# Rotary latent queries of two head groups from one product of 512 columns instead of two products of 256

## The chip, the cores and the metric

The kernel runs on one core of a Trainium2 chip, as one launch. The metric is the device time of that launch in microseconds (us); lower is better. The engines are named as in the profile: PE does matmuls (PEld is its loading of the stationary operand), DVE is the vector engine, ACT the activation engine, POOL and SP issue transfers here and do little else. Each engine works through its own queue in order, and semaphores order the queues among each other.

## The reference

A decoder trunk of four layers over 256 tokens of width 2048, in float32. Layers 0 and 3 use multi-head latent attention, layer 1 a sparse attention with an indexer, layer 2 a windowed attention with sinks. Every layer has one input projection, four memory cross-attention heads of width 256, a SiLU gate over the whole branch of 3072 columns, and one output projection that is added to the residual. What matters here is the query side of the latent layers:

```python
c_q, c_kv, k_rope, mq, gate = _split(h @ w_in, [A_Q_LORA, A_KV_LORA, A_ROPE, MEM_WIDTH, BRANCH_WIDTH])
q = (_rmsnorm(c_q, q_norm) @ w_uq).reshape(B, S, A_HEADS, A_NOPE + A_ROPE)      # 16 heads of 128 + 64
kv = (_rmsnorm(c_kv, kv_norm) @ w_ukv).reshape(B, S, A_HEADS, A_NOPE + A_V)     # 16 heads of 128 + 128
q_nope, q_rope = q[..., :A_NOPE], _rope(q[..., A_NOPE:])
s = (einsum('bqhd,bkhd->bhqk', qn, k_nope) + einsum('bqhd,bkd->bhqk', qr, k_rope)) * scale
```

`A_Q_LORA` is 1536, so the query projection runs over 12 feature tiles of 128. Of the 192 columns of `w_uq` of each head the first 128 are plain, the last 64 are rotated by position (`_rope`).

## The kernel before

Float32 products are made of three products in PE's faster 32-bit format (`float32r`): every operand is split into a high part and the remainder, and high by high, high by low and low by high are summed in PSUM. Weights are loaded by SP in `stage` (one of five buffers `wr`), then split in `parts_of`: ACT copies the high part `wh` (line 60), DVE subtracts for the low part `wl` (line 64), three buffers each. Two functions make the products:

- `rows_by` (lines 234 to 236): the activations are stationary, the weights move; the result has tokens on the partitions and up to 512 columns. Six matmuls per feature tile: two row tiles of 128 tokens by three products.
- `columns_by` (lines 253 and 257): the weights are stationary, the activations move.

A latent layer first builds the compressed queries and keys (`first`: acc_kva, acc_kvb, acc_cq; the result is `cT`). Then it goes through six parts in the order 4, 0, 1, 2, 3, 5: parts 4 and 5 are memory heads (`memory_project`, `memory_attend`), parts 0 to 3 are groups of four latent heads. For a group g, `project(g)` makes in this order

1. the rotary queries acc_qr (`rows_by`, 12 feature tiles, 4 heads x 64 = 256 columns), which DVE rotates from PSUM (`rope`, lines 508 to 511, with the single buffer `rot`), ACT and DVE split into `qrs` (a single buffer), PE transposes (line 370, tile `tr`) and ACT copies to `qrT`,
2. the plain queries acc_qn (two halves by `columns_by`, evacuated by `head_parts`), 
3. the keys acc_kn (two halves), the values acc_va (`rows_by`, 512 columns),
4. the group's quarter of the gate, acc_g (two halves by `columns_by` over 16 feature tiles).

`attend` then makes for each of the four heads the scores (line 625, tile `sp`; the rotary part `sp<-kr,qrT` is among them), the softmax, its transposes (line 402, `ptp`) and the product with the values (lines 406 and 407, `o`). `w_out` of the part before follows (acc_wo, lines 234 to 236).

That is the program's order. The order on each engine's queue is set by a scheduler that runs at build time over a modelled timeline, and that moves pieces of one part among those of another: the softmax of one group lies among the first products of the next. Tiles come from pools with a tag and a number of buffers: accumulators `acc` (4, a product takes two), `aux` (3: `qrT`, the values `va`, the loaded memory values `mvr`, and others), `pq` (5), `wr` (5). POOL issues the loads `mvr` and `mkr` of stored memory values and keys. SP issues one transfer per feature tile for a column pattern with gaps, as for acc_qr (pieces of 64 floats, 256 B).

Of the kernel before, what the change touches and what calls it, by code (L numbers as in the profile page):

```python
# [8 lines left out]
F32 = mybir.dt.float32  # L9
F32R = mybir.dt.float32r  # L10
# [5 lines left out]
P = 128  # L16
S = 256
# [6 lines left out]
A_QL, A_KVL, A_ROPE, A_NOPE = 1536, 512, 64, 128  # L24
MEMW = 1024
ST = 2
N_TAB = 384
PQ, AUX, WR = 5, 3, 5


@with_exitstack
def kernel(ctx: ExitStack, tc: tile.TileContext, a: dict, out: bass.AP,
                             kinds=(0, 1, 2, 0)):
    nc = tc.nc
# [3 lines left out]
    act = ctx.enter_context(tc.tile_pool(name="act", bufs=1))  # L38
    wk = ctx.enter_context(tc.tile_pool(name="wk", bufs=1))
# [3 lines left out]
    def misc(name, dt=F32):  # L43
        return ps.tile([P, 512], dt, name=name, tag="mp", bufs=4)
# [8 lines left out]
    def f32(ap):  # L53
        return ap.bitcast(F32)
# [4 lines left out]
    def copy_act(o, i, scale=1.0):  # L59
        nc.scalar.activation(o, i, AF.Copy, scale=scale)  # L60

    def split(hi, lo, src):
        copy_act(hi, src)
        nc.vector.tensor_sub(lo, src, f32(hi))  # L64
# [135 lines left out]
    def stage(w, k0, m, cols):  # L200

        n = cols[1] if len(cols) == 2 else cols[1] * cols[4]
        wr = wp.tile([P, ST * 512], F32, name="wr", tag="wr", bufs=WR)
        src = w[k0 * P:(k0 + m) * P, :].rearrange("(k p) n -> p k n", p=P)
        dst = wr[:, :m * n].rearrange("p (k n) -> p k n", k=m)
        if len(cols) == 2:
            nc.sync.dma_start(dst, src[:, :, cols[0]:cols[0] + n])
        else:
            c0, r, step, off, width = cols
            for k in range(m):  # L210
                nc.sync.dma_start(dst[:, k, :].rearrange("p (r c) -> p r c", r=r),
                                  src[:, k, c0:c0 + r * step].rearrange("p (r c) -> p r c", r=r)
                                  [:, :, off:off + width])
        return wr, n

    def parts_of(wr, c0, n):
        wh = wp.tile([P, 512], F32R, name="wh", tag="wh", bufs=3)
        wl = wp.tile([P, 512], F32R, name="wl", tag="wl", bufs=3)
        split(wh[:, :n], wl[:, :n], wr[:, c0:c0 + n])
        return wh, wl  # L220

    def rows_by(xt, kts, w, k0, cols, name):

        acc = [ps.tile([P, 512], F32, name=f"acc_{name}{t}", tag="acc", bufs=4) for t in range(2)]
        for s in range(0, kts, ST):
            m = min(ST, kts - s)
            wr, n = stage(w, k0 + s, m, cols)
            for k in range(m):
                wh, wl = parts_of(wr, k * n, n)
                q = xt[(s + k) // 4]  # L230
                for t in range(2):
                    xh, xl = (q[:, v, (s + k) % 4, t * P:(t + 1) * P] for v in range(2))
                    first, last = s + k == 0, s + k == kts - 1
                    nc.tensor.matmul(acc[t][:, :n], xh, wh[:, :n], start=first, stop=False)  # L234
                    nc.tensor.matmul(acc[t][:, :n], xh, wl[:, :n], start=False, stop=False)  # L235
                    nc.tensor.matmul(acc[t][:, :n], xl, wh[:, :n], start=False, stop=last)  # L236
        return acc

    def columns_by(xt, kts, w, k0, cols, name):

        acc = [ps.tile([P, 2, S], F32, name=f"acc_{name}{j}", tag="acc", bufs=4) for j in range(2)]
        for s in range(0, kts, 2 * ST):
            m = min(2 * ST, kts - s)
            wr, n = stage(w, k0 + s, m, cols)
            for k2 in range(0, m, 2):
                wh, wl = parts_of(wr, k2 * S, 2 * S)
                for k in range(2):
                    kt = s + k2 + k
                    q = xt[kt // 4]

                    for j in range(2):
                        o = k * S + j * P
                        nc.tensor.matmul(acc[j], wh[:, o:o + P], q[:, :, kt % 4, :],  # L253
                                         start=kt == 0, stop=False)
                    for j in range(2):
                        o = k * S + j * P
                        nc.tensor.matmul(acc[j][:, 0, :], wl[:, o:o + P], q[:, 0, kt % 4, :],  # L257
                                         start=False, stop=kt == kts - 1)
        return acc

    def total(acc, name="z"):
        z = wk.tile([P, S], F32, name=name, tag="z", bufs=3)
        copy_act(z, acc[:, 1, :])
        nc.vector.tensor_add(z, z, acc[:, 0, :])  # L264
        return z
# [98 lines left out]
    def transposed(dst, srcs):  # L364

        for i0 in range(0, len(srcs), 4):
            i1 = min(len(srcs), i0 + 4)
            tp = misc("tr", F32R)
            for i in range(i0, i1):
                nc.tensor.transpose(tp[:, (i - i0) * P:(i - i0 + 1) * P], srcs[i], identr)  # L370
            copy_act(dst(i0, i1), f32(tp)[:, :(i1 - i0) * P].rearrange("p (j c) -> p j c", c=P))


    def gate(nm, w, c0):
        gT = act.tile([P, 4, S], F32, name="gT", tag="gT", bufs=2)
        for h in range(2):
            acc = columns_by(nm.at, 16, w, 0, (c0 + h * S, S), "g")
            for j in range(2):
                z = total(acc[j])
                hz = wk.tile([P, S], F32, name="hz", tag="z", bufs=3)  # L380
                nc.vector.tensor_mul(hz, z, nm.half)
                th = wk.tile([P, S], F32, name="th", tag="e", bufs=4)
                nc.scalar.activation(th, hz, AF.Tanh)
                nc.vector.scalar_tensor_tensor(gT[:, 2 * h + j, :], th, 1.0, hz, op0=OP.add, op1=OP.mult)
        return gT
# [117 lines left out]
    def rope(dst, src, t, n):  # L503

        cb = cos[:, t, None, :].to_broadcast([P, n, A_ROPE])
        q = A_ROPE // 2
        rot = wk.tile([P, 4, A_ROPE], F32, name="rot", tag="rot", bufs=1)[:, :n]
        nc.vector.tensor_mul(rot[:, :, :q], src[:, :, q:], sin[:, t, None, :q].to_broadcast([P, n, q]))
        nc.vector.tensor_mul(rot[:, :, q:], src[:, :, :q], sin[:, t, None, q:].to_broadcast([P, n, q]))
        nc.vector.tensor_mul(dst, src, cb)  # L510
        nc.vector.tensor_add(dst, dst, rot)


    class Latent:
# [6 lines left out]
        def first(self):  # L521
# [55 lines left out]
            for z, sg in zip(self.scale, (1.0, -1.0)):  # L577
                nc.vector.tensor_scalar(z, qr, sg * (A_NOPE + A_ROPE) ** -0.5, None, op0=OP.mult)

        def project(self, g):  # L580

            j = self.j
            wq, wkv = a["w_uq"][j], a["w_ukv"][j]
            qn, kn = [], []
            qr = act.tile([P, 4, S], F32R, name="qrT", tag="aux", bufs=AUX)
            v = act.tile([P, 2, 512], F32, name="va", tag="aux", bufs=AUX)
            acc = rows_by(self.cT[:3], 12, wq, 0, (g * 768, 4, 192, A_NOPE, A_ROPE), "qr")
            for t in range(2):
                rr = wk.tile([P, 4, A_ROPE], F32, name="qrr", tag="z", bufs=3)
                rope(rr, acc[t][:, :S].rearrange("p (h d) -> p h d", h=4), t, 4)  # L590
                rs = wk.tile([P, 4, 2, A_ROPE], F32R, name="qrs", tag="qrs", bufs=1)
                split(rs[:, :, 0, :], rs[:, :, 1, :], rr)
                transposed(lambda i0, i1: qr[:, i0:i1, t * P:(t + 1) * P],
                           [rs[:, h].rearrange("p a b -> p (a b)") for h in range(4)])
            for half in range(2):
                acc = columns_by(self.cT[:3], 12, wq, 0, (g * 768 + half * 384, 2, 192, 0, A_NOPE), "qn")
                q = act.tile([P, 2, 2, S], F32R, name="qn", tag="pq", bufs=PQ)
                head_parts(q, acc)
                qn.append(q)
            for half in range(2):  # L600
                acc = columns_by(self.cT[3:], 4, wkv, 0, (g * 1024 + half * 512, 2, 256, 0, A_NOPE), "kn")
                k = act.tile([P, 2, 2, S], F32R, name="kn", tag="pq", bufs=PQ)
                head_parts(k, acc)
                kn.append(k)
            acc = rows_by(self.cT[3:], 4, wkv, 0, (g * 1024, 4, 256, A_NOPE, A_NOPE), "va")
            for t in range(2):
                copy_act(v[:, t, :], acc[t])
            return qn, qr, kn, v, gate(self.nm, self.w, self.g0 + g * 512)

        def attend(self, qn, qr, kn, v, gT):  # L610
            y = act.tile([P, 2, 4, S], F32R, name="y", tag="y", bufs=2)
# [288 lines left out]
```

## Time and profile before

| what | us |
|---|---|
| median of 3 runs | 2638.45 (2636.72 to 2638.67) |
| the profiled execution's own time | 2637.23 |
| its span, from the first to the last instruction | 2635.0 |
| PE busy | 2605.1 |
| DVE busy | 1890.2 |
| ACT busy | 1625.5 |
| POOL busy | 57.8 |

The span is what the trace covers; the own time also holds what lies around it. Busy time of PE counts overlapping matmuls once. In the views, a row `L236 PE MATMUL acc_qr<-wh,cT` is line 236 of the kernel, the engine, the operation, and the tiles written and read; `x` stands ahead of a count, and in a view by order of time the first two numbers are the start and the duration in us. The product names of the text (acc_qr and so on) are those tiles.

### The profile page before, as it was taken

The numbers are of one execution on the slowest core, as the hardware profiler recorded it, in microseconds if no ns is written. First come the engines' busy times: TensorE is split into PE (matmuls) and PEld (weight loads), VectorE is DVE, ScalarE is ACT, GpSimd is POOL, SyncE is SP. The second block draws the span as 40 slices with busy tenths as digits, with TensorE's granted clock in tenths as the row PEclk, the third lists the DMA queues.
The fourth block names the chain that finished last, engine by engine and source line by source line (L and its number), as shares of the span: only waits on it lengthen the run. The fifth ranks groups of instructions, "written<-read, shape, count | busy, mean of one in ns | idle before, by whom it ended". The sixth has DMA issues, their size and how long they took to land.

```text
span 2635.0 us, 43048 instructions
## 1 busy us (share of the span) xinstructions
PE 2605.1 (99%) x14623; PEld 2260.1 (86%) x14623; DVE 1890.2 (72%) x4174; ACT 1625.5 (62%) x3460; POOL 57.8 (2%) x102
## 2 busy tenths in 40 slices
PE   8999999999999999999999999999999999999998
PEld 7888888888888889888888888888888888888886
DVE  7566656677767685877777776777778767776767
ACT  6455556556656566666666666676666655665655
POOL 1000000000000000000000000000000000000000
PEclk9999999999999999999999999999999999999999
DMA  7898886666557666565556665555555766665764
GB/s 268 272 290 275 273 265 199 165 187 168 169 160 224 192 189 171 167 183 170 175 164 190 188 191 176 173 172 177 191 168 162 206 163 188 165 171 156 226 183 135
DMA packets 454064, 507.50 MB, mean 193 GB/s; under 512 B 69300, under 2 KB 352180, under 8 KB 452692
## 3 DMA queue, kind: packets, MB, share of 16 engines
q1 hardware_dynamic: 439716, 446.42, 57.3%
q0 software_dynamic: 13120, 56.17, 6.7%
q8 instruction: 115, 1.88, 0.3%
q10 hardware_dynamic: 1008, 2.16, 0.2%
q14 instruction: 105, 0.86, 0.1%
HBM read 485.70 MB, written 31.56 MB: 196 GB/s over the span
## 4 chain that ended last, share of the span: by engine, by line
PE 97%; DMA 1%; DVE 1%; ACT 0%; issue 0%; ACTq 0%; POOLq 0%
PE acc_g L253 14%; PE acc_g L257 7%; PE acc_wo L234 7%; PE acc_wo L235 7%; PE acc_wo L236 7%; PE acc_mq L253 5%; PE acc_mk L253 5%; PE acc_qn L253 3%; PE acc_cq L253 3%; PE acc_mq L257 2%; PE acc_mk L257 2%; PE acc_q L234 2%; PE acc_q L235 2%; PE acc_q L236 2%; PE acc_mv L235 2%; PE acc_mv L236 2%
## 5 line engine op out<-in xcount | busy, mean ns | idle before, releaser
L64 DVE TENSOR_TENSOR wl<-wr,wh 128x512 fp32r<-128x512 f32 (+2 forms) x1776 | 1172.9, 663 | 642.9 <-ACT wh L60 612.7
L60 ACT ACTIVATE wh<-wr 128x512 fp32r<-128x512 f32 (+2 forms) x1776 | 1079.9, 609 | 846.1 <-PE acc_g L253 186.0
L253 PE MATMUL acc_g<-xT,wh 128*128 128x512 f32 x1536 | 488.9, 397 | 0.6 <-DVE z L264 0.6
L257 PEld LDWEIGHTS acc_g<-xT,wl 128*128 128x128 f32 x1536 | 285.2, 188 | 60.7
L257 PE MATMUL acc_g<-xT,wl 128*128 128x256 f32 x1536 | 311.0, 280 | 0.0
L235 PE MATMUL acc_wo<-wl,y 128*128 128x512 f32 x768 | 302.5, 394 | 0.6 <-DVE wl L64 0.5
L236 PE MATMUL acc_wo<-wh,y 128*128 128x512 f32 x768 | 299.1, 390 | 0.0
L253 PEld LDWEIGHTS acc_g<-xT,wh 128*128 128x128 f32 x1536 | 238.1, 189 | 4.7 <-issue 1.1
L234 PE MATMUL acc_wo<-wh,y 128*128 128x512 f32 x768 | 240.4, 393 | 0.7 <-ACT wh L60 0.6
L235 PEld LDWEIGHTS acc_wo<-wl,y 128*128 128x128 f32 x768 | 144.3, 188 | 30.0 <-DVE wl L64 1.4
L236 PEld LDWEIGHTS acc_wo<-wh,y 128*128 128x128 f32 x768 | 144.2, 188 | 28.4
L234 PEld LDWEIGHTS acc_wo<-wh,y 128*128 128x128 f32 x768 | 141.3, 188 | 27.8 <-ACT wh L60 1.0
L253 PE MATMUL acc_mk<-mT,wh 128*128 128x512 f32 x512 | 160.8, 396 | 1.4 <-ACT wh L60 1.4
L253 PE MATMUL acc_mq<-xT,wh 128*128 128x512 f32 x512 | 161.7, 397 | 0.0
L807 DVE TENSOR_TENSOR x<-x,acc_wo 128x512 f32<-128x512 f32 x192 | 125.5, 681 | 7.2 <-PE acc_wo L236 6.9
L253 PE MATMUL acc_qn<-cT,wh 128*128 128x512 f32 x384 | 123.2, 399 | 0.0
L253 PE MATMUL acc_cq<-xT,wh 128*128 128x512 f32 x384 | 120.8, 396 | 0.0
L257 PEld LDWEIGHTS acc_mk<-mT,wl 128*128 128x128 f32 x512 | 95.8, 188 | 22.7 <-DVE wl L64 0.4
L257 PEld LDWEIGHTS acc_mq<-xT,wl 128*128 128x128 f32 x512 | 93.7, 188 | 20.0
L257 PE MATMUL acc_mq<-xT,wl 128*128 128x256 f32 x512 | 102.5, 281 | 0.0
L235 PE MATMUL acc_q<-wl,xT 128*128 128x512 f32 x256 | 102.4, 400 | 0.0
L257 PE MATMUL acc_mk<-mT,wl 128*128 128x256 f32 x512 | 100.8, 278 | 0.0
(284 smaller groups left out, 4453.5 us busy)
## 6 DMA issues: line engine op xcount, KB each, us to landing
wr<-in_w_out_dram SPq DMA_DIRECT2D x192, 512.0 KB, 3.7
wr<-in_w_in_a_dram SPq DMA_DIRECT2D x176, 512.0 KB, 4.2
wr<-in_w_mem_kv_dram SPq DMA_DIRECT2D x128, 512.0 KB, 5.2
wr<-in_w_in_b_dram SPq DMA_DIRECT2D x112, 512.0 KB, 3.7
wr<-in_w_in_c_dram SPq DMA_DIRECT2D x104, 512.0 KB, 3.7
wr<-in_w_uq_dram SPq DMA_DIRECT2D x288, 128.0 KB, 2.8
tab<-flat POOLq DMA_DIRECT2D x8, 1536.0 KB, 10.9
wr<-in_w_in_a_dram SPq DMA_DIRECT2D x32, 288.0 KB, 3.0
```

The source lines that it names most:

```text
L60: nc.scalar.activation(o, i, AF.Copy, scale=scale)
L64: nc.vector.tensor_sub(lo, src, f32(hi))
L234: nc.tensor.matmul(acc[t][:, :n], xh, wh[:, :n], start=first, stop=False)
L235: nc.tensor.matmul(acc[t][:, :n], xh, wl[:, :n], start=False, stop=False)
L236: nc.tensor.matmul(acc[t][:, :n], xl, wh[:, :n], start=False, stop=last)
L253: nc.tensor.matmul(acc[j], wh[:, o:o + P], q[:, :, kt % 4, :], start=kt == 0, stop=False)
L257: nc.tensor.matmul(acc[j][:, 0, :], wl[:, o:o + P], q[:, 0, kt % 4, :], start=False, stop=kt == kts - 1)
L807: nc.vector.tensor_add(xs, xs, acc[t])
```

## The change

The rotary queries of two neighbouring groups (0 and 1, 2 and 3) are made by one call of `rows_by` with 8 heads x 64 = 512 columns per feature tile. It is a function of its own, `rotary`, which `project` calls for even groups, behind the plain queries, the keys and the values and ahead of the gate. Rotation, split, transposes and copies stay the same for each group and row tile. Two tiles `qrT` now live at once, and the pool `aux` has five buffers instead of three; a scratch for the descriptors of POOL's transfers is set to 8192 bytes.

```diff
-PQ, AUX, WR = 5, 3, 5
+PQ, AUX, WR = 5, 5, 5
...
+        def rotary(self, g):
+
+            self.qr = [act.tile([P, 4, S], F32R, name="qrT", tag="aux", bufs=AUX) for z in range(2)]
+            acc = rows_by(self.cT[:3], 12, a["w_uq"][self.j], 0, (g * 768, 8, 192, A_NOPE, A_ROPE), "qr")
+            for t in range(2):
+                for z in range(2):
+                    rr = wk.tile([P, 4, A_ROPE], F32, name="qrr", tag="z", bufs=3)
+                    rope(rr, acc[t][:, z * S:(z + 1) * S].rearrange("p (h d) -> p h d", h=4), t, 4)
+                    rs = wk.tile([P, 4, 2, A_ROPE], F32R, name="qrs", tag="qrs", bufs=1)
+                    split(rs[:, :, 0, :], rs[:, :, 1, :], rr)
+                    transposed(lambda i0, i1: self.qr[z][:, i0:i1, t * P:(t + 1) * P],
+                               [rs[:, h].rearrange("p a b -> p (a b)") for h in range(4)])
+
         def project(self, g):
...
-            qr = act.tile([P, 4, S], F32R, name="qrT", tag="aux", bufs=AUX)
             v = act.tile([P, 2, 512], F32, name="va", tag="aux", bufs=AUX)
-            acc = rows_by(self.cT[:3], 12, wq, 0, (g * 768, 4, 192, A_NOPE, A_ROPE), "qr")
-            for t in range(2):
-                rr = wk.tile([P, 4, A_ROPE], F32, name="qrr", tag="z", bufs=3)
-                rope(rr, acc[t][:, :S].rearrange("p (h d) -> p h d", h=4), t, 4)
-                rs = wk.tile([P, 4, 2, A_ROPE], F32R, name="qrs", tag="qrs", bufs=1)
-                split(rs[:, :, 0, :], rs[:, :, 1, :], rr)
-                transposed(lambda i0, i1: qr[:, i0:i1, t * P:(t + 1) * P],
-                           [rs[:, h].rearrange("p a b -> p (a b)") for h in range(4)])
...
             for t in range(2):
                 copy_act(v[:, t, :], acc[t])
-            return qn, qr, kn, v, gate(self.nm, self.w, self.g0 + g * 512)
+            if g % 2 == 0:
+                self.rotary(g)
+            return qn, self.qr[g % 2], kn, v, gate(self.nm, self.w, self.g0 + g * 512)
...
-    nc = _bacc.Bacc("TRN2", target_bir_lowering=False, num_devices=1)
+    nc = _bacc.Bacc("TRN2", target_bir_lowering=False, num_devices=1,
+                     dynamic_dma_scratch_size=8192)
```

## The prediction

> **What bounds the kernel now.** I read the page first, then the waits of PE, then the busy time of the two stretches in which the rotary queries lie (layers 0 and 3, the latent ones).
>
> ```profile
> span 2635.0 us, 43048 instructions
> PE 2605.1 (99%) x14623; PEld 2260.1 (86%) x14623; DVE 1890.2 (72%) x4174; ACT 1625.5 (62%) x3460; POOL 57.8 (2%) x102
> ...
> PE 97%; DMA 1%; DVE 1%; ACT 0%; issue 0%; ACTq 0%; POOLq 0%
> ```
>
> ```profile
> PE acc_kvb L234 <- ACT wh L60: 1.8, 1, 1.8
> PE o L786 <- ACT pT L60: 1.7, 3, 0.6
> ```
>
> ```profile
> core 0: us, PE busy (x) PEld busy (x) DVE busy (x) ACT busy (x) POOL busy (x), PEclk, DMA share, GB/s
> 395.00:940.00 545.00, 545.00 (x3176) 479.31 (x3176) 385.27 (x863) 331.77 (x698) 3.57 (x6) 1.00 0.64 183
> ```
>
> PE is busy 99% of the span, and 97% of the chain that ended last is PE. No single wait of PE after the first loads is longer than the 1.8 us on acc_kvb, early in layer 0, before any rotary query. In the 545 us from there to the end of layer 0 PE is busy in all 545.00, at a granted clock of 1.00. So in the stages that change there is no idle time to win, and whatever shortens PE's own list shortens the span one to one, as long as no other engine or transfer becomes late. Busy time counts overlapping matmuls as one, so the price of a matmul is read from start to start, in the order of time.
>
> **The products, which are the gain.** A latent layer has four head groups, two layers make eight. Before, each has 12 feature tiles x 2 row tiles x 3 products (high by high, high by low, low by high) of 256 columns:
>
> ```profile
> L234 PE MATMUL acc_qr<-wh,cT x192: 277/283/368, 519.9 to 2444.9; 128*128 128x256 f32 x192
> L235 PE MATMUL acc_qr<-wl,cT x192: 278/283/387, 520.1 to 2445.2; 128*128 128x256 f32 x192
> L236 PE MATMUL acc_qr<-wh,cT x192: 277/283/287, 520.2 to 2445.4; 128*128 128x256 f32 x192
> ```
>
> These are 576 matmuls. After, four calls of 72, which is 288 matmuls of 512 columns. The start-to-start time of the first kind is read where nothing else stands between; of the second kind acc_va is the nearest row: same function, same lines, same operand layout, 512 columns, weights in blocks from the same kind of load.
>
> ```profile
> 797.08 0.40 PE L234 MATMUL acc_qr<-wh,cT 128*128 128x256 f32 x2
> ...
> 799.96 0.63 PE L253 MATMUL acc_qn<-cT,wh 128*128 128x512 f32 x2
> ```
>
> ```profile
> 736.61 0.63 PE L234 MATMUL acc_va<-wh,cT 128*128 128x512 f32 x2
> ...
> 741.40 0.62 PE L253 MATMUL acc_g<-xT,wh 128*128 128x512 f32 x2
> ```
>
> From 797.08 to 799.96 stand 24 matmuls (four feature tiles of six): 2.88 / 24 = 0.120 us. From 736.61 to 741.40 stand 21: 4.79 / 21 = 0.228 us. So 576 x 0.120 = 69.1 us become 288 x 0.228 = 65.7 us: **-3.4 us**. Two halves cost 0.240 where one whole costs 0.228; one matmul of 256 saved is worth 12 ns. As the upper bound for 512 columns I take acc_g's pair among halves, 0.235 (0.47 us for two, from 760.20 on, below), which would leave -1.4 us; the other way, both intervals are read to 0.01 us over 20 and more matmuls, which is worth 0.3 us: -3.7 us.
>
> The second PE term is the stretch behind transposes and products in plain f32:
>
> ```profile
> 776.39 0.49 PE L402 MATMUL ptp<-ident,e 128*128 128x128 f32 x3
> 776.63 0.48 PE L235 MATMUL acc_wo<-wl,y 128*128 128x512 f32 x1
> 776.95 0.39 PE L236 MATMUL acc_wo<-wh,y 128*128 128x512 f32 x1
> ```
>
> The first matmul behind a group of ptp takes 0.32 to the next instead of 0.23. In the built order of the changed kernel the softmax of the group before is spread differently (its ptp, o and sp now fall among acc_qn and acc_kn), and there are 178 such places behind ptp for 180, equally many behind o (32) and behind transposes of rotary and other parts (78). 2 x 0.09: **-0.2 us**. PE's order outside the latent projections is the same instruction by instruction.
>
> Sum: **-3.6 us** on the profiled execution's 2637.23 us (2635.0 us span and 2.2 around it). That run lies 1.2 us under the median of the runs shown, 2638.45, to which the same difference applies: 2634.8 us, 0.14% less. A measurement of this kernel tells about 0.2%, 5.3 us, from no change.
>
> **What costs nothing, and what covers it.**
> - The splits of the weights: 96 pairs of 256 columns on ACT and DVE become 48 of 512, slightly less work on engines that are 62% and 72% busy; cover is PE.
> - The rotation. Still 16 calls, but four in a row instead of two, at the start of the gate, with single buffers `rot` and `qrs`. DVE shows how such a row runs in the kernel before:
>
> ```profile
> 800.22 0.28 DVE L508 TENSOR_TENSOR rot<-acc_qr,sin 128x128 f32<-128x128 f32 x1
> 800.42 0.28 DVE L509 TENSOR_TENSOR rot<-acc_qr,sin 128x128 f32<-128x128 f32 x1
> 800.62 0.41 DVE L510 TENSOR_TENSOR qrr<-acc_qr,cos 128x256 f32<-128x256 f32 x1
> 800.95 0.68 DVE L64 TENSOR_TENSOR wl<-wr,wh 128x512 fp32r<-128x512 f32 x1
> 801.55 0.42 DVE L511 TENSOR_TENSOR qrr<-qrr,rot 128x256 f32<-128x256 f32 x1
> ...
> 803.82 0.42 DVE L64 TENSOR_TENSOR qrs<-qrr,qrs 128x256 fp32r<-128x256 f32 x1
> 804.16 0.68 DVE L390 TENSOR_TENSOR yt<-o,gT 128x512 f32<-128x512 f32 x1
> ```
>
> ```profile
> 760.20 0.63 PE L253 MATMUL acc_g<-xT,wh 128*128 128x512 f32 x2
> 760.67 0.39 PE L257 MATMUL acc_g<-xT,wl 128*128 128x256 f32 x2
> 760.90 0.62 PE L253 MATMUL acc_g<-xT,wh 128*128 128x512 f32 x2
> ```
>
> From start to start a rotation and its split take 0.20 + 0.20 + 0.33 + 0.34 + 0.34 = 1.41 us of DVE, a split of weights 0.60. In the built order the first four transposes stand 34 gate matmuls behind the last rotary product, the next ones 22 to 24 apart; a gate matmul takes 0.70 / 4 = 0.175 us, so 5.9 us and then 3.9 to 4.2 us. DVE needs 4.0 us for the first (800.22 to 804.16, with four other pieces among them) and 1.41 + 3 x 0.60 = 3.2 us for each further one. It fits, with 0.7 us to spare at the tightest. In the kernel before, the first transposes also stand 34 matmuls behind, and PE does not wait there.
> - The accumulators: two pairs in all; the rotary pair is read until the fourth rotation (about 7.6 us of DVE), and the gate's second half, which takes that pair, comes 64 matmuls, 11 us, later.
> - SP's queue: the 96 issues of 128 KB become 48 of 256 KB, and stand behind those of kn and va instead of ahead of those of qn; bytes and pieces (256 B) stay the same.
> - POOL's queue: five `aux` buffers let the memory values `mvr` of some parts be issued earlier, by pairs; the smaller DMA scratch touches POOL's transfers alone, and POOL is busy for 57.8 us of the span. Loads that then collide with those of the weights have the five `wr` buffers as cover; without that the price is a wait like the 1.8 us on acc_kvb (below).
>
> **The rivals.**
>
> *The 256-byte pieces cannot keep pace* (slower). A feature tile now takes 6 x 0.228 = 1.37 us of PE for 256 KB, 192 GB/s, all in pieces of 256 B, for 12 tiles in a row.
>
> ```profile
> 776.00:778.00 2.00, 2.00 (x12) 1.65 (x11) 1.35 (x3) 1.28 (x3) 0.00 (x0) 1.00 0.57 128
> 778.00:780.00 2.00, 2.00 (x11) 1.66 (x10) 0.81 (x2) 1.11 (x2) 0.00 (x0) 1.00 0.58 131
> 510.00:511.00 1.00, 1.00 (x8) 0.91 (x7) 0.96 (x4) 0.90 (x3) 0.00 (x0) 1.00 1.00 227
> ```
>
> Over 2 us such pieces have gone at no more than 128 to 131 GB/s, but at a DMA share of 0.57 and 0.58, since the buffers asked for no more; in the one microsecond at a share of 1.00 it was 227. If 131 were the limit, 12 x 262 KB would take 24.0 us; the first load can be issued when the last one of qn is split, 11 us ahead of its use (kn and va), of which some 2 us go to splits that run ahead; the last of the six loads would land at about 2 + 24 = 26 us, and is wanted at 9.1 + 5 x 2.74 = 22.8 us: 3.2 us late, four times, 13 us, so 2634.8 + 13 = 2648 us. It decides below 3.15 MB / (22.8 - 2) = 151 GB/s. The 227 speaks against it. [...]
>
> *The chain of rotations ends late* (no gain). If ACT's half of the split or its copies come in unlucky order, PE waits at each of the 16 groups of transposes; 0.25 us each, about what the spare 0.7 us would leave if it were overdrawn by a third, gives +4 us, and 2638.8 us. It decides when a rotation with its three splits takes over 3.9 us. Against it: the same spacing without waits before.
>
> [...]
>
> *More than the products is won* (faster). The 1.8 us wait on acc_kvb comes from POOL's loads:
>
> ```profile
> 381.11 0.53 POOL L351 DMA_DIRECT2D mkT<-mkT  x1 [10.05 <-DVE mkT L64]
> 381.63 1.07 POOL L455 DMA_DIRECT2D mvr<-mv  x2
> 382.68 0.56 POOL L458 DMA_DIRECT2D mkr<-mkT  x1
> ```
>
> ```profile
> 391.87 0.78 ACT L60 ACTIVATE wh<-wr 128x288 fp32r<-128x288 f32 x2 [2.21 <-DMA wr<-in_w_in_a_dram]
> ```
>
> Three transfers of 512 KB go out at once, and the split of weights that follows waits 2.21 us for its own load, PE 1.8 us for the split. With five `aux` buffers the two `mvr` no longer wait for stores of memory values; were they issued some 10 us earlier, the wait would go: -3.6 - 1.8 = -5.4 us, 2633.0 us, and with the products that run slow behind the wait perhaps 2631. It decides if `mvr` gets ahead of the store of mkT. Against it: in POOL's built order it still stands behind that store, which waits for DVE. The other places where `mvr` now goes earlier have no wait on PE to give back.
>
> **How the numbers follow.** Forecast 0.54: 2634.8 us, with 2633 to 2637 as its own range (the bounds of the 512 columns, and 1 us for the scatter of the runs shown, 2636.72 to 2638.67). Faster rival 0.20, chain 0.10, a product that saves nothing 0.03, 256-byte pieces 0.13. The range 2631 to 2641 takes in the forecast, the faster rival and both cases without gain, and leaves out the 2648. Faster by over 0.2% (under 2633.2): the faster rival and 0.05 of the forecast, 0.25. Slower by over 0.2% (over 2643.7): the pieces, and 0.03 of the chain where it costs twice that: 0.16. Within: 0.59.
>
> **What would show it.** In the profile after, acc_qr as 96 matmuls of 512 columns on each of L234, L235 and L236, at 0.228 us from start to start, and PE still busy in all of layer 0 and layer 3. DMA would show itself as ACT waiting for `wr<-in_w_uq_dram` in the rotary product or at the gate's first load; the chain as PE waiting for `qrs` at `tr`; the faster rival as the wait on acc_kvb gone. The forecast is wrong if the 512-column products take 0.24 us, or if PE's idle time in the two layers is over 3 us.

## The result and the profile after

The changed kernel takes 2634.8 us (median of 22 runs, 2632.54 to 2637.3), the kernel before 2638.26 us in the same comparison (22 runs). The ratio is 0.9988, with a 95% interval from 0.9982 to 0.9993: 3.5 us or 0.13% faster, less than the 0.2% bound of the prediction, and still clear of no change over so many runs.

The page of the kernel after, first the span, busy times and the chain that ended last:

```profile
span 2633.5 us, 42188 instructions
PE 2603.5 (99%) x14335; PEld 2247.5 (85%) x14335; DVE 1883.7 (72%) x4126; ACT 1621.4 (62%) x3412; POOL 57.8 (2%) x102
...
PE 97%; DMA 1%; DVE 1%; ACT 0%; issue 0%; ACTq 0%; POOLq 0%
```

PE has 288 matmuls fewer (14623 to 14335) and is still the bound, with the same shares. The rotary products, by their tile, and the same products by order of time:

```profile
L234 PE MATMUL acc_qr<-wh,cT x96: 389/389/389, 555.1 to 2391.1; 128*128 128x512 f32 x96
L235 PE MATMUL acc_qr<-wl,cT x96: 389/389/389, 555.5 to 2391.8; 128*128 128x512 f32 x96
L236 PE MATMUL acc_qr<-wh,cT x96: 389/389/389, 555.7 to 2392.0; 128*128 128x512 f32 x96
```

```profile
557.77 0.61 PE L234 MATMUL acc_qr<-wh,cT 128*128 128x512 f32 x2
...
571.38 0.61 PE L253 MATMUL acc_g<-xT,wh 128*128 128x512 f32 x2
```

Between these two rows stand ten feature tiles of six matmuls: 13.61 / 60 = 0.227 us each. So 288 x 0.227 = 65.4 us stand where 576 x 0.120 = 69.1 us stood, 3.7 us less. Layer 0 by its busy time, and what PE waited for over the whole span:

```profile
395.00:940.00 545.00, 545.00 (x3036) 473.63 (x3036) 381.75 (x838) 330.32 (x675) 4.64 (x8) 1.00 0.65 185
```

```profile
PE gp L91 <- DMA rows<-in_mem_norm_dram: 7.4, 1, 7.4
PE acc_kvb L234 <- ACT wh L60: 3.1, 1, 3.1
PE o L792 <- ACT pT L60: 1.7, 3, 0.6
```

PE (the second number of the row, ahead of its count) is busy in all 545.00 us, and no wait has come at the weights, the transposes or the gate. One wait has grown, that on acc_kvb, from 1.8 to 3.1 us. It hides part of the gain in this pair of profiles: their spans differ by only 1.5 us (2635.0 and 2633.5). By the starts of the matmuls the two latent stretches (layer 0 from its first acc_cq on, and layer 3) take 1196.9 us before and 1193.2 after, 3.7 less, which is what the products give. The way from the first acc_kvb to the first acc_cq grows from 16.4 to 18.7 us, which takes 2.3 back: 1.3 is the longer wait, and the rest is behind it. Stretches by engine, the granted TensorE clock third from the end, of the kernel before and then of the kernel after:

```profile
395.00:396.00 1.00, 1.00 (x6) 1.00 (x6) 0.16 (x1) 0.34 (x1) 0.00 (x0) 0.50 0.53 183
396.00:397.00 1.00, 1.00 (x9) 1.00 (x8) 0.46 (x1) 0.40 (x2) 0.00 (x0) 0.97 0.71 136
```

```profile
398.00:399.00 1.00, 1.00 (x6) 1.00 (x5) 0.24 (x1) 0.44 (x1) 0.00 (x0) 0.50 0.63 211
400.00:401.00 1.00, 1.00 (x10) 1.00 (x9) 0.52 (x2) 0.56 (x2) 0.00 (x0) 1.00 0.55 91
```

After the wait the clock is granted at 0.50, and a microsecond holds 6 matmuls of acc_kvb and not 10. By the clock records of the traces it is granted at half from 392.64 to 396.06 us before and from 392.61 to 399.43 after, 3.41 and 6.83 us. PE had work for 3.4 and 5.9 us of these, so about 1.7 and 2.9 us were lost, some 1.2 more, which is the rest to within 0.2 us. In these two profiles the stretches between two changes of the clock are whole multiples of 3.413 us (3.41 is one, 6.83 two, and the 382.29 us ahead of the fall in the kernel before are 112). The fall came some 2.1 us after the last matmul ahead of the wait in both (390.5 to 392.6), and in the kernel before PE had been idle for only 1.8 us of these. The experiments below show that wait and clock vary from one profile to the next.

### The profile page after: what moved, and what is told of

Read it like the earlier page. It is cut to its first block, busy times and chain, and to the rows that moved or that the text cites. A ratio compares the mean times of both kernels' runs of the same rounds, so it can differ in the third digit from the quotient of the medians.

```text
span 2633.5 us, 42188 instructions
## 1 busy us (share of the span) xinstructions
PE 2603.5 (99%) x14335; PEld 2247.5 (85%) x14335; DVE 1883.7 (72%) x4126; ACT 1621.4 (62%) x3412; POOL 57.8 (2%) x102
## 4 chain that ended last, share of the span: by engine, by line
PE 97%; DMA 1%; DVE 1%; ACT 0%; issue 0%; ACTq 0%; POOLq 0%
PE acc_g L253 14%; PE acc_g L257 7%; PE acc_wo L234 7%; PE acc_wo L235 7%; PE acc_wo L236 7%; PE acc_mq L253 5%; PE acc_mk L253 5%; PE acc_qn L253 3%; PE acc_cq L253 3%; PE acc_mq L257 2%; PE acc_mk L257 2%; PE acc_q L234 2%; PE acc_q L235 2%; PE acc_q L236 2%; PE acc_mv L235 2%; PE acc_mv L236 2%
```

## The experiments

The question is whether the number of matmuls is the gain, or one of the other things that changed with it: the place, the pools, the larger loads. Its rival inside the profile is the wait on acc_kvb.

**The products cut in half again.** Everything as in the changed kernel, but each product is two matmuls:

```diff
-                    nc.tensor.matmul(acc[t][:, :n], xh, wh[:, :n], start=first, stop=False)
...
+                    for c0 in range(0, n, cut):                      # cut=256, acc_qr only
+                        cs = slice(c0, min(n, c0 + cut))
+                        nc.tensor.matmul(acc[t][:, cs], xh, wh[:, cs], start=first and c0 == 0, stop=False)
...
```

> The changed kernel with one thing undone: each rotary product of 512 columns is issued as two matmuls of 256 columns (576 matmuls in all, as before), in the same place, from the same loads, splits and five aux buffers. If the number of matmuls is the gain: 576 x 0.120 us again, so all 3.5 us are lost and the time is that of the kernel before, 2638.3 us, ratio 1.000, with 0.120 us from start to start. If place, order, larger loads or wider splits are the gain: 2634.8 us, ratio 0.9987, like the changed kernel.

2638.24 us, ratio 0.9999 (0.9991 to 1.0008): the whole gain is gone. Its products by order of time:

```profile
555.75 0.40 PE L236 MATMUL acc_qr<-wh,cT 128*128 128x256 f32 x2
...
557.18 0.40 PE L236 MATMUL acc_qr<-wh,cT 128*128 128x256 f32 x2
```

Twelve matmuls in 1.43 us, 0.119 us each. Place, loads, splits and buffers are those of the changed kernel, and none of them is the gain. The latent stretches say the same: 1197.1 us, against 1196.9 before and 1193.2 after.

**The place undone.** `rotary` is called first in `project` of an even group, with its 512 columns.

```diff
             qn, kn = [], []
+            if g % 2 == 0:
+                self.rotary(g)
...
-            if g % 2 == 0:
-                self.rotary(g)
             return qn, self.qr[g % 2], kn, v, gate(self.nm, self.w, self.g0 + g * 512)
```

> The changed kernel with the place undone: the product of 512 columns stands first among the projections of an even group, where the products of 256 stood before; everything else as changed. If the number of matmuls is the gain: 2634.8 us, ratio 0.9987. If the place behind the values matters: near 2638 us, ratio 1.000, with waits of PE at the transposes or the weights.

2634.94 us, ratio 0.9989 (0.998 to 0.9998): in time not to be told from the changed kernel. The profile sees a little more: the latent stretches take 1193.8 us, 0.6 more than in the changed kernel and 3.1 less than before. So 0.6 of the 3.7 us hang on where the wide product stands, which the times of the runs are too coarse to tell.

**The pools alone.** The kernel before with the two constants of the change:

```diff
-PQ, AUX, WR = 5, 3, 5
+PQ, AUX, WR = 5, 5, 5
...
+                     dynamic_dma_scratch_size=8192)
```

> The kernel before with nothing but the pool sizes changed: five aux buffers, and 8192 bytes of scratch for POOL's descriptors. PE's order is that of before. If the number of matmuls is the gain: 2638.3 us, ratio 1.000. If earlier loads of memory values are the gain: 2634.8 us. If they are a loss that hides a larger gain of the products (the wait on acc_kvb was 3.1 us in the changed kernel's profile against 1.8 us): 2639.6 us and the wait on acc_kvb again near 3 us.

2638.0 us, ratio 0.9999 (0.999 to 1.0008): no gain and no loss. The wait on acc_kvb, in this kernel's profile and then in that of the kernel with the place undone:

```profile
PE acc_kvb L234 <- ACT wh L60: 2.3, 1, 2.3
```

```profile
PE acc_kvb L234 <- ACT wh L60: 3.0, 1, 3.0
```

With 1.8 before and 3.1 after, four kernels with the same work at that place wait between 1.8 and 3.1 us, one profile each; whether the build or the single execution makes the difference is not shown. That a larger `aux` makes it longer is not shown: it was 2.3 here, with five. Nor does the clock always fall behind it. This kernel's stretch around the wait:

```profile
388.00:402.00 14.00, 11.69 (x87) 11.27 (x86) 6.37 (x15) 6.96 (x17) 0.00 (x0) 1.00 0.90 281
```

The granted clock is 1.00 over it, with a wait longer than that of the kernel before, behind which it fell. In this profile it fell elsewhere, from 135.20 to 138.62 us, behind a wait of 1.6 us on acc_mk. What decides it is not shown; the length of the wait alone does not.

**Cut in four.** `cut=128` in place of 256, 1152 matmuls.

> The changed kernel with each rotary product issued as four matmuls of 128 columns: 1152 matmuls in the place of 288. If a matmul costs its columns and a fixed 13 ns (0.227 for 512, 0.120 for 256): 128 columns take 0.066 us, 1152 x 0.066 = 76 us, 11 us more than changed, 2645.5 us. If the loading of the stationary operand sets a floor near 0.11 us, as between the 128-column rows of the value products of the sparse layers (o<-pT,vz): 1152 x 0.11 = 127 us, 62 us more, 2697 us; the 13 ns would then not have to be a cost of every matmul. [...]

2697.51 us, ratio 1.0225 (1.0211 to 1.0239). By order of time:

```profile
552.77 0.28 PE L237 MATMUL acc_qr<-wl,cT 128*128 128x128 f32 x1
...
554.89 0.28 PE L236 MATMUL acc_qr<-wh,cT 128*128 128x128 f32 x1
```

Nineteen steps in 2.12 us, 0.112 us for 128 columns, hardly less than for 256. So "columns and a fixed 12 or 13 ns", which gives 0.066 us here, is not the cost of a matmul of any width; a floor of about 0.11 us for each matmul of these products would fit, an estimate from this run.

**Cut at 320.** One matmul of 320 and one of 192 columns, to tell a floor per matmul from a lower rate for narrow ones.

> The changed kernel with each rotary product issued as one matmul of 320 columns and one of 192: 288 of each. The four quarters took 0.111 us each where columns and 13 ns would be 0.066. If the floor is a time per matmul: 320 columns at 0.147 us (as columns and 13 ns), 192 at 0.111 us, together 74.3 us, 8.9 us more than changed, 2643.7 us. If instead columns under 256 run at half rate: 192 at 0.16 to 0.17 us, together 89 us, 23 us more, 2658 us. If columns and 13 ns held for 192 as well: 0.093 us, 69 us, 3.7 us more, 2638.5 us.

2643.64 us, ratio 1.0021 (1.001 to 1.0031), 8.8 us above the changed kernel and where the floor puts it (2643.7).

```profile
554.99 0.31 PE L237 MATMUL acc_qr<-wl,cT 128*128 128x320 f32 x1
555.13 0.31 PE L238 MATMUL acc_qr<-wh,cT 128*128 128x320 f32 x1
555.28 0.25 PE L236 MATMUL acc_qr<-wh,cT 128*128 128x192 f32 x1
555.37 0.28 PE L237 MATMUL acc_qr<-wl,cT 128*128 128x192 f32 x1
555.48 0.27 PE L238 MATMUL acc_qr<-wh,cT 128*128 128x192 f32 x1
555.60 0.33 PE L237 MATMUL acc_qr<-wl,cT 128*128 128x320 f32 x1
```

The steps tell more than the sum: 320 columns take 0.14 to 0.15 us; the first 192 takes 0.09, the second 0.11, the third 0.12. The first narrow matmul behind wide ones passed in 0.09 us, which is what columns and 13 ns give for 192 (0.093), and the next two took more. From these steps I estimate that something needs 0.11 us for each matmul and gets ahead during wide ones; no run shows it by itself. The loading of the stationary operand, which PE does once for each matmul (14335 matmuls and as many loads, PEld, in the kernel after), is the candidate that the profile offers. The transposes of the rotary queries speak for it: they too have 128 columns, but their loads are shorter, and inside a group of four they follow each other at 0.06 to 0.09 us (median 0.065). The loads, of the kernel before:

```profile
L234 PEld LDWEIGHTS acc_qr<-wh,cT x192: 187/189/192, 519.8 to 2444.8; 128*128 128x128 f32 x192
L370 PEld LDWEIGHTS tr<-identr,qrs x64: 137/141/146, 545.0 to 2456.8; 128*128 128x128 f32 x64
```

So 0.11 us is not the floor of every matmul of 128 columns. But a transpose differs from a product in more than its load, and no run took the load away from these products, so that it is the cause is not shown.

**The pieces of 256 bytes, twice.** Each transfer of the rotary weights is issued again into a buffer that is not read:

```diff
+                if twice:                                            # acc_qr only
+                    again = wk.tile([P, 512], F32, name="again", tag="hl", bufs=3)
+                    nc.sync.dma_start(again.rearrange("p (r c) -> p r c", r=r), ...)
```

> The changed kernel, and every transfer of the rotary weights is issued a second time, into a buffer that nothing reads: 24 x 262 KB of 256-byte pieces in a rotary stage instead of 12. The demand is 385 GB/s over the products. If such pieces go at 227 GB/s at most: 27.7 us, the last load lands some 7 us late, in each of four stages, 28 us more, 2663 us, with ACT waiting for wr<-in_w_uq_dram. If the limit were 131 GB/s: 48 us, 27 us late each time, 2743 us. If the limit is far higher, or the lead longer than worked out: 2635 us.

2638.57 us, ratio 1.0002 (0.9993 to 1.0011): 3.8 us above the changed kernel, and none of the expected 28. The table of transfers, then two stretches inside a rotary stage (the last two numbers of a row are DMA share and GB/s):

```profile
again<-in_w_uq_dram SPq DMA_DIRECT2D x48, 256.0 KB, 6.6
...
wr<-in_w_uq_dram SPq DMA_DIRECT2D x48, 256.0 KB, 3.8
```

```profile
726.00:727.00 1.00, 1.00 (x8) 0.87 (x7) 1.00 (x4) 1.00 (x2) 0.00 (x0) 1.00 1.26 284
730.00:732.00 2.00, 2.00 (x11) 1.65 (x10) 1.67 (x4) 0.90 (x2) 0.00 (x0) 1.00 1.17 246
```

Such pieces go at 284 GB/s over one microsecond and 246 over two; the 227 that I took for a limit was none, and the 192 that the change asks for stay below both. (Per share of the engines they do carry less: 284 GB/s at 1.26, where the kernel after had 384 at 1.08 at 391 us, when pieces of 288 columns came in.) PE waited for nothing in either latent layer from acc_cq on, and the latent stretches take 1193.2 us, as in the changed kernel. So the 3.8 us of the median do not lie in the rotary products. The profile, of the fastest of the ten executions (2636.14), holds only 0.6 of them; its waits differ ahead of layer 0:

```profile
PE acc_mk L258 <- ACT wh L60: 2.7, 2, 2.4
PE acc_kvb L239 <- ACT wh L60: 2.1, 1, 2.1
```

PE waits 2.7 us on acc_mk here, against 1.1 in the kernel after, in the memory stage before any rotary product, and the first acc_kva starts at 380.1 instead of 376.1 us; the shorter wait on acc_kvb and the clock, which does not fall behind it here, give most of that back. Why the memory stage ran less evenly in this build stays open.

**The loads of the first memory values moved behind acc_kvb.** In the changed kernel POOL issues three transfers of 512 KB at 381 us, while the narrow loads for acc_kva and acc_kvb run. In layer 0 the tiles of these transfers, and of the first keys that went out at 370 us, get a one-column write that depends on the key norm:

```diff
+            if late:                                                 # layer 0, part 4
+                nc.vector.tensor_copy(v[z][:, 0, :1], kvr_[0][:, :1])
             nc.gpsimd.dma_start(v[z], mv[i][part][:, z])
...
```

> The changed kernel, and in layer 0 the loads of the first stored memory values and keys wait for the key norm (a one-column write into their tiles), so that they come after acc_kvb instead of at its start. If their collision with the weights makes the wait on acc_kvb and the slow products behind it (3.1 us and some 3 more in the profile): both go, 2630 us, ratio 0.997. If the wait has another cause: 2634.8 us and the wait stays. A loss, over 2636 us, if the memory heads then wait for their values.

2630.04 us, ratio 0.997 (0.9958 to 0.9981), 4.8 us below the changed kernel. POOL and the waits of PE:

```profile
411.86 1.07 POOL L458 DMA_DIRECT2D mvr<-mv  x2 [30.15 <-DVE mkr L462]
```

```profile
PE gp L91 <- DMA rows<-in_mem_norm_dram: 7.2, 1, 7.2
PE o L800 <- ACT pT L60: 1.7, 3, 0.6
PE ptp L402 <- ACT e L60: 1.4, 3, 0.5
PE acc_mk L253 <- ACT wh L60: 1.3, 1, 1.3
```

The wait on acc_kvb is gone. 4.8 us is more than the wait itself (1.8 to 3.1): the clock behind it does not fall either. The same stretch of this kernel, and then of the kernel after:

```profile
388.00:402.00 14.00, 14.00 (x108) 13.91 (x107) 8.31 (x18) 9.02 (x21) 0.00 (x0) 1.00 0.81 236
```

```profile
388.00:402.00 14.00, 10.90 (x63) 10.68 (x62) 4.49 (x11) 5.11 (x12) 0.00 (x0) 0.76 0.73 234
```

A granted clock of 1.00 and no idle time, against 0.76 and 3.1 us. That the transfers collide is seen in the queues' shares of the DMA engines from 386 to 388 us, ahead of the wait; q0 carries the loads that POOL issued, q1 those of the weights. The kernel after, and then this one (packets, MB, share):

```profile
q0 software_dynamic: 170, 0.64, 94.9%
q1 hardware_dynamic: 16, 0.02, 3.9%
```

```profile
q1 hardware_dynamic: 342, 0.37, 86.1%
```

In these two microseconds the weights got 16 packets beside POOL's loads, and 342 without them.

**The same in the kernel before**, with 256 columns and three `aux` buffers.

> The kernel before, with two products of 256 columns and three aux buffers, and with the late loads of layer 0 alone. If the gain of the products and that of the late loads are independent: 2638.3 - 4.8 = 2633.5 us, ratio 0.9982. If the late loads only work with five aux buffers: 2638.3 us.

2634.22 us, ratio 0.9986 (0.9977 to 0.9995), 4.1 us below its own kernel. The two gains add up, and the late loads need neither the wide product nor the larger pool.

**The copies of the bias tables one by one.** On top of the late loads; two of the eight copies went out together in the second memory step.

```diff
-                for c in copies[:2 if step == 1 else 1]:
+                for c in copies[:1]:
```

> The kernel with the late loads of layer 0, and the table copies by POOL spread over the memory steps one by one instead of two together in the second step. If the two copies together delay the weights and so make the wait of PE on acc_mk near 133 us (1.1 to 1.6 us, with 0.5 to 1 us of slow products): 2628.5 us, ratio 0.9963, that wait gone. If a single copy delays them as well: 2630 us and the wait stays or moves.

2633.79 us, ratio 0.9984 (0.9975 to 0.9993): 3.8 us worse than without. The wait on acc_mk went, and another is back:

```profile
380.56 0.53 POOL L151 DMA_DIRECT2D tab<-flat  x1
```

```profile
PE acc_kvb L234 <- ACT wh L60: 3.7, 1, 3.7
```

The eighth copy now falls to the eighth step, at 380.56 us, into the very gap from which the memory values were taken. With that copy put behind the late loads:

```diff
+                for c in copies[:1 if step < 7 else 0]:
...
+        if late:
+            table_copies(1, 3)
```

> The kernel with the late loads of layer 0, the table copies one by one in seven memory steps, and the eighth copy behind the late loads. If POOL's transfers at the turn to layer 0 are what delays the weights for acc_kvb, whichever they are: both the wait there and the one on acc_mk are gone, 2628.5 us, ratio 0.9963. If the eighth copy was not what brought the wait back: 2633.8 us, as with the copies one by one.

2628.43 us, ratio 0.9962 (0.9948 to 0.9976), 9.9 us under the kernel before; this is the best version that was run. Its five executions lie within 0.5 us (2628.02 to 2628.55), the 21 of the kernel before beside them within 3.4 (2636.8 to 2640.21), so that most of the scatter seems to have come from these two waits and the clock behind them. Neither wait is left:

```profile
PE gp L91 <- DMA rows<-in_mem_norm_dram: 7.5, 1, 7.5
PE o L802 <- ACT pT L60: 1.7, 3, 0.6
PE ptp L402 <- ACT e L60: 1.4, 3, 0.5
```

**All profiles by stretch**, worked out from the starts of the matmuls (us, one execution each). The latent stretches are layer 0 from the first acc_cq to the first product of layer 1 (acc_iq), and layer 3 from its first acc_kva to the last matmul; between the two lie 1019.4 to 1019.5 us in all of them. The last column is the time at half clock around acc_kvb.

| kernel | first acc_kva | from there to acc_cq | latent stretches | half clock |
|---|---|---|---|---|
| before | 376.2 | 29.0 | 1196.9 | 3.41 |
| pools alone | 378.4 | 28.1 | 1197.0 | 0 |
| before, late loads | 376.6 | 25.3 | 1197.0 | 0 |
| after | 376.1 | 31.3 | 1193.2 | 6.83 |
| 256-byte pieces twice | 380.1 | 27.9 | 1193.2 | 0 |
| late loads | 376.2 | 25.3 | 1193.2 | 0 |
| late loads, copies one by one | 375.1 | 30.6 | 1193.2 | 3.41 |
| late loads, eighth copy behind | 374.9 | 25.3 | 1193.2 | 0 |
| place undone | 376.9 | 31.3 | 1193.8 | 6.83 |
| cut in half | 377.0 | 28.2 | 1197.1 | 0 |
| cut at 320 | 376.9 | 30.1 | 1202.7 | 3.41 |
| cut in four | 376.2 | 28.0 | 1256.9 | 0 |

Kernels with the same rotary products at the same place agree to 0.1 us in the latent stretches. All else that differs lies ahead of acc_cq, and from acc_kva to there it is 25.3 us each time that none of POOL's large transfers meets these loads.

## Why the prediction came out

- **The bound.** Right: PE's own list set the span, and the saving on it passed to the span one to one over the comparison (3.5 us; 3.4 when the halves are put back; 3.7 by the latent stretches).
- **The products.** Forecast -3.4 us, from 0.228 us for 512 columns; measured 0.227, so -3.7 us. acc_va was the right row to take: same function and operands. The first nine of its 21 matmuls stand behind a change of kinds and run at 0.230 us, the other twelve at 0.227, as acc_qr in a block of its own.
- **Stretch behind transposes.** -0.2 us is not there. The latent stretches lose 3.7 us in all, which the products alone give, and with the halves put back at the new place they are 0.2 us longer than before. So the sum of -3.6 us is in part luck: the products were put 0.3 us too low, and this term took 0.2 the other way. The mechanism and the main term do not hang on it.
- **What was to cost nothing.** The rotations are covered, the accumulators free in time, the larger loads in time: PE does not wait at any of them. The pools were neutral (2638.0 us alone).
- **The 256-byte pieces.** The rival had 0.13 and would have cost 13 us. With the demand doubled, such pieces reached 284 GB/s and PE's rotary stages did not wait at all. The error was to read a rate at a DMA share of 1.00 as a ceiling: the share went to 1.26. The 0.13 was my own estimate; no run shows a limit of 131 GB/s for such pieces, and the trace shows no harm from them at this demand.
- **A product that saves nothing** (no gain from the wider product, 0.03, my own estimate). The halves settle it: 576 matmuls against 288 are worth 3.4 us in time, everything else equal. The 12 ns are real between 256 and 512 columns; as a cost of any matmul they are wrong, since 128 columns of these products take 0.112 us.
- **The faster rival.** Its mechanism was right, its condition was not met, and its price was too low. The loads did not move: in the kernel after, POOL issues them at 381.52 us, behind the store, as the built order had said. Moved by hand they gave 4.8 us, where I had counted 1.8 and "perhaps" two more for slow products; what made them slow, the half clock behind the wait, and that it lasted 6.83 us in one profile where it lasted 3.41 in the other, was not seen.
- **The step that was weak** is the reading of one profile as if it were the median: the wait on acc_kvb differs by a microsecond and more among the profiles, and the two profiled executions by their whole time alone would have shown half of the gain.

## What to carry to other kernels

Where PE is busy in a whole stage, price a change of its list from start to start in blocks of one kind, and look for a row of the same function and operands for the new width: that gave the main term to 0.3 us, although the result is only 0.13%. A gain of that size is shown by undoing one part at a time in many runs, and by comparing the stretch that changed from start to start, not by the whole time of two profiles. And the larger gain lay beside the change: transfers that PE first read 108 and 154 us after their issue (the keys and the values of the kernel after), issued as soon as their queue was free, took 94.9% of the DMA engines over 2 us in which the narrow loads that PE needed next got 3.9%; hold such transfers back by a dependence, and check which other transfer then moves into the gap.

## What the runs showed of the hardware that I had not expected

- A stream of matmuls of these 32-bit products takes 0.227 us at 512 columns, 0.119 to 0.120 at 256, and 0.112 at 128: for these products, half of 256 columns saved only 0.007 to 0.008 us. Behind wide ones, the first 192-column matmul passed in 0.09 us; transposes of 128 columns, whose loads are shorter (0.141 us, not 0.189), follow each other at 0.065.
- Pieces of 256 B came in at 284 GB/s over a microsecond, where the kernel before had asked for 128 and 131 over the two stretches of 2 us shown.
- Three transfers of 512 KB, or a single table copy of 1.5 MB, issued while loads of 288 columns run, cost PE a wait of 1.8 to 3.7 us. POOL's loads had 94.9% of the DMA engines over two microseconds, those of the weights 3.9%. Taking the cause away was worth 4.1 to 5.4 us in all.
- Behind a wait of 1.8 and one of 3.1 us the granted clock was 0.50 for 3.41 and 6.83 us, behind one of 2.3 us it stayed at 1.00. In the profiles before and after, its changes lay whole multiples of 3.413 us apart (1, 2, 111, 112, 652 and 653).
